# A two-layer hybrid block on one core: gram heads side by side, value products in pairs of key tiles, norm squares by halves, broadcasts by transposes, new stream shares

## The chip, the core and the metric

The kernel runs on one core of a Trainium2 chip. TensorE (PE) multiplies, VectorE (DVE), ScalarE (ACT) and GpSimd (POOL) work elementwise, SyncE (SP) issues the DMAs. The metric is the device time of one execution in microseconds; lower is better. A "clock" is the share of its full 2.4 GHz that TensorE was granted in a stretch.

## What is computed

Two layers over 1,280 tokens (256 of a context, 1,024 latents) of width 1,024, all in float32. Each layer is a modulated RMS norm, one projection w_in into four mixers that see the same tokens, the projection w_out, a second norm and an MLP. Cut to what matters here:

```python
def _rms(x, g):
    y = x * lax.rsqrt(jnp.mean(jnp.square(x), axis=-1, keepdims=True) + EPS)
    return y * g

def gated_delta_rule(q, k, v, g, beta, s0):        # 4 heads of 64, chunks of 64, two directions
    decay = jnp.exp(jnp.where(tri, gc[..., :, None] - gc[..., None, :], -jnp.inf))
    a = jnp.where(strict, jnp.einsum('bhncd,bhnsd->bhncs', k * beta, k) * decay, 0.0)
    t_inv = triangular_solve(a + eye, eye)
    u, w = t_inv @ (v * beta), t_inv @ (k * beta * jnp.exp(gc))
    qk = jnp.where(tri, jnp.einsum('bhncd,bhnsd->bhncs', q, k) * decay, 0.0)
    ...                                            # scan over chunks: v_new = u - w @ s, o = q @ s + qk @ v_new

def _attend(q, k, v):                              # mla: 4 heads, 96 wide, values 64 wide
    p = softmax(jnp.einsum('bqhd,bkhd->bhqk', q, k) * (MLA_QK ** -0.5))
    return jnp.einsum('bhqk,bkhd->bqhd', p, v)

for l in range(DEPTH):
    a = _modulate(h, norm1_g[l], m[0], m[1]) @ w_in[l]
    ya, yb, yc, yd = gdn_mixer(a), s5_mixer(a), mamba2_mixer(a), mla_mixer(a)
    h = h + m[2] * (concatenate([ya, yb, yc, yd]) @ w_out[l])
    h = h + m[5] * _sq_relu_mlp(_modulate(h, norm2_g[l], m[3], m[4]), w_ff1[l], w_ff2[l])
```

The products `q k` and `k k` of the delta rule are called grams below, and the triangular solve is done by a base inverse of 16 x 16 blocks followed by merges.

## The kernel before

**Streams.** The program is written as generators. `Streams.run` always steps the one whose own clock `at` is smallest; a step adds the estimated cost of what it issued, divided by the stream's share:

```python
s = min(ok, key=lambda s: s.at)
...
s.at += (self.work[0] + 20) / s.share
```

The shares stand in the table `SHARE` (lines 147 to 151); a higher share lets a stream get further in the same time. The order that comes out is the order of each engine's queue (a tile framework adds the waits); each engine works its queue in order. Since every instruction is issued through one helper, all carry its line, L125, and groups are told apart by the names of their tiles.

**The main stream** runs per layer: `w_in1` and `w_in2` (projections, weights split into a high and a low part, three products per tile: `a_hi,w_hi`, `a_lo,w_hi`, `a_hi,w_lo`), `ssd`, `mla`, then `s5` if nobody has begun it, then it waits for the side stream, and runs `w_out` and `ffn`. **The side stream** (`beside`, line 1914) starts with share `prep0` and does the small per-token factors, `gdn_prep` of the first pair of heads, then `gdn`: for each of two head pairs the grams and base inverse (`base`), the merges and the scan chains of both directions (`solve`), and at the end `s5`. So the delta rule is interleaved with projections, ssd and mla.

**Banks.** TensorE writes into PSUM banks, named by who uses them: two `mm`, one each of `g`, `x`, `m0`, `m1`, `c0`, `c1`. In the trace `m` and `c` are those of the two directions together. The merges use only `m`, the chains `c`; the base uses `m` and `c` in turn.

**What the change touches:**
- `gram` (481): an exponent of the decay in one bank; then per head `hl` a bank, two products of 64-row operands `qk[hs]` (one per tile of the pair), two scalings on VectorE, and a yield. Base and chain call it, the chain at 646 with three times its bank c.
- `gdn_prep` (415), `ssd` (783), `norm_scale` (1600): a row of per-token factors (`g_cx`, `s_rr`, `n_rr`) is spread over 128 partitions by a product with the identity, `mm(b, x, ident)`.
- `norm_scale`: per 128 tokens ScalarE squares 1,024 rows into `n_sq` (8 x 128 per partition), VectorE sums the eight by one reduce into `n_acc`, TensorE sums over partitions.
- `att` in `mla_att` (1094): per key tile six score products (two heads, three products) into a bank, an exponent on ScalarE into `m_p` (three buffers), running sums on GpSimd, and, two tiles behind, two value products `x<-m_p,m_va` into 64 rows each of the bank `x`. `fin` (1129) sums `m_sum` over partitions and divides.
- `s5`'s output writes `yd`, reads it as `5_yf`, multiplies by `5_wg`, and puts `5_mo` into the mixers' buffer `mx`, from which `w_out` loads `f_mx`.

A matrix product on float32 operands is two records in the trace, a transpose (`tr`) one.

Of the kernel before, what the change touches and what calls it, by code (L numbers as in the profile page):

```python
# [7 lines left out]
F32 = mybir.dt.float32  # L8
# [4 lines left out]
OP = mybir.AluOpType  # L13
AX = mybir.AxisListType
# [99 lines left out]
class Engine:  # L114
# [14 lines left out]
    def cost(self, op, aps):  # L129
# [4 lines left out]
        if self.name == "tensor":  # L134
# [12 lines left out]
SHARE = {"start": 1.2612, "norm": 8.885, "mod": 0.7917, "tables": 2.1733, "conv": 0.1457, "ffn": 5.4917,  # L147
# [3 lines left out]
         "chain": 1.0205, "heads": 1.2072, "scan": 1.1114, "factors": 1.7425}  # L151
# [58 lines left out]
class Core:  # L210
# [204 lines left out]
    def gdn_prep(self, l, getP, hp, pool, p1, G, bk):  # L415

        nc, A, S, c = self.nc, self.A, self.S, self.c
# [21 lines left out]
        for x in range(2):  # L439
# [4 lines left out]
            for t0, n in ((0, 2), (2, 4), (6, 4)):  # L444
                b = self.bank(bk)
                for j in range(n):
                    self.mm(b[:, j * 128:j * 128 + 128], rnx[:, t0 + j].rearrange("p h e -> p (h e)"), c["ident"])
# [14 lines left out]
    def gdn(self, l, getP, put, G, bk, ctx_out=True, side="right"):  # L462
# [18 lines left out]
        def gram(hp, d, qk, p2, x, tags, pool, dtag, dst=None):  # L481
# [19 lines left out]
            yield  # L501
            for hl in range(2):
                g = self.bank(next(tag))
                hs = slice(64 * hl, 64 * hl + 64)
                for i in range(2):
                    oi = o + 128 * i
                    self.mm(g[:, 128 * i:128 * i + 128], qk[hs, 0, oi:oi + 128], qk[hs, x, oi:oi + 128])
                for i in range(2):
                    be = S["beta"][:, t + i, 4 * d + 2 * hp + hl:4 * d + 2 * hp + hl + 1]
                    nc.vector.scalar_tensor_tensor(dst[:, i, hl], g[:, 128 * i:128 * i + 128], be, D[:, i, hl],  # L510
# [124 lines left out]
        def chain(hp, d, p2, V, wT, st, ot, pool, seen):  # L635
# [9 lines left out]
            if t in tiles:  # L645
                qg = yield from gram(hp, d, qk, p2, 1, (f"c{d}",) * 3, pool, f"g_Dq{d}")
# [136 lines left out]
    def ssd(self, l, getP, conv, put, pool, bk, ctx_out=True):  # L783
# [110 lines left out]
        for t0, n in ((0, 2), (2, 4), (6, 4)):  # L894
# [3 lines left out]
            for j in range(n):  # L898
                self.mm(b[:, j * 128:j * 128 + 128], rr[:, t0 + j:t0 + j + 1].to_broadcast([128, 128]), c["ident"])
# [132 lines left out]
    def mla_att(self, put, wk, qt, kt, va, gq, ctx_out, bk, sk, ak):  # L1032
# [61 lines left out]
        def att():  # L1094
            for i in range(2 * len(blocks)):
# [5 lines left out]
                ps = {}  # L1101
                for k in range(nk + 2):
                    if k < nk:
# [7 lines left out]
                        ps[k] = self.t(wk, [128, 512], F32, "m_p", bufs=3)  # L1111
# [3 lines left out]
                    if k == 2 and pend:  # L1115
                        fin(*pend.pop(), acc[:, 256:512])
                    if k >= 2:
                        for x in range(2):
# [993 lines left out]
```

## Time and profile before

| | |
|---|---|
| three runs | 4422.18, 4426.31, 4437.6 us (median 4426.31) |
| the profiled execution | 4413.32 us, span 4411.5 us, mean granted clock 0.919 |
| busy: TensorE, VectorE, GpSimd, ScalarE | 89%, 62%, 33%, 29% of the span |
| layer 0: w_in beside the delta rule | about 300 to 745 us |
| layer 0: ssd | about 745 to 950 us |
| layer 0: mla | about 950 to 1356 us |
| layer 0: w_out, norm, MLP | 1377 to about 2380 us |
| layer 1: mixers, then w_out and MLP | about 2500 to 3580, and 3580 to 4411 us |

Busy time is what the engine spent in instructions; a stretch's clock says how fast TensorE's were. What an engine does alone costs its duration, what it does while the next one is waiting for something else costs nothing; the chain of waits says which engine held up the end at each moment.

### The profile page before, as it was taken

Reading aid. Unit: us, or ns where it says so; the run is one execution under the profiler, and the core shown is the slowest. Engines: PE = TensorE matmul, PEld = TensorE weight load, DVE = VectorE, ACT = ScalarE, POOL = GpSimd, SP = SyncE. Lnnn points to the kernel's source line nnn. Section 1 sums busy time; section 2 is a strip of 40 time slices with the busy share of each in tenths; the row PEclk is TensorE's granted clock in tenths of the full one; section 3 lists DMA queues with packets and bytes.
Section 4 is the critical chain, followed back from the end, with each engine's and each line's share of the span. In section 5 each row is a group of like instructions: output and inputs, shape, how many; then the busy total and the mean of one; then the engine's idle time right before and its main releaser. Section 6 shows DMA issues by size and latency. Waiting matters only on the chain.

```text
span 4411.5 us, 61602 instructions
## 1 busy us (share of the span) xinstructions
PE 3920.8 (89%) x23416; PEld 3135.9 (71%) x23416; DVE 2713.7 (62%) x6343; ACT 1275.3 (29%) x2027; POOL 1449.0 (33%) x1664
## 2 busy tenths in 40 slices
PE   4689897898887899999999799897978998999999
PEld 2466786675665778877788677776855666888887
DVE  7866555756554599997775655576765436444443
ACT  3224235332223321112222343234322233212121
POOL 3432532434452221123332224334435432212121
PEclk8899996787898999999999999996979998999999
DMA  4346333010335022311111233342041230111111
GB/s 184 119 158 188 113 123 104 1 45 3 77 106 174 29 86 96 101 63 54 63 56 56 86 133 104 102 145 67 8 109 35 66 137 29 53 44 54 42 58 58
DMA packets 170872, 367.30 MB, mean 83 GB/s; under 512 B 46160, under 2 KB 88400, under 8 KB 166864
## 3 DMA queue, kind: packets, MB, share of 16 engines
q1 hardware_dynamic: 170576, 363.37, 25.5%
q8 instruction: 184, 3.01, 0.3%
q14 instruction: 112, 0.92, 0.1%
HBM read 277.42 MB, written 85.89 MB: 82 GB/s over the span
## 4 chain that ended last, share of the span: by engine, by line
PE 62%; DVE 23%; POOL 6%; issue 3%; ACT 3%; DMA 2%; SPq 0%; POOLq 0%; DVEq 0%; ACTq 0%
PE mm L125 43%; PE m L125 7%; PE c L125 5%; PE g L125 4%; PE x L125 3%; DVE mod_acc L125 3%; DVE h L125 2%; DVE n_x L125 1%; DVE s_ca L125 1%; DVE 5_t_k L125 1%; POOL g_pr L125 1%; DVE n_acc L125 1%; DVE g_scr L125 1%; POOL a_lo L125 1%; DVE rsq_u L125 1%
## 5 line engine op out<-in xcount | busy, mean ns | idle before, releaser
L125 PE MATMUL mm<-a_hi,w_hi 128*128 128x512 f32 (+1 forms) x2576 | 979.2, 381 | 54.6 <-ACT w_hi L125 20.8
L125 PE MATMUL mm<-a_lo,w_hi 128*128 128x512 f32 (+1 forms) x2576 | 970.3, 377 | 31.9 <-POOL a_lo L125 19.3
L125 PE MATMUL mm<-a_hi,w_lo 128*128 128x512 f32 (+1 forms) x2576 | 964.3, 375 | 1.2 <-POOL w_lo L125 1.2
L125 POOL TENSOR_TENSOR w_lo<-w_raw,w_hi 128x1024 fp32r<-128x1024 f32 x189 | 464.4, 2466 | 1225.7 <-ACT w_hi L125 1225.7
L125 DVE SCALAR_TENSOR_TENSOR h<-mm,md,h 128x512 f32<-128x512 f32 (+1 forms) x680 | 467.2, 692 | 255.1 <-PE mm L125 254.2
L125 PEld LDWEIGHTS mm<-a_hi,w_hi 128*128 128x128 f32 x2576 | 499.4, 194 | 146.9 <-ACT w_hi L125 21.3
L125 PEld LDWEIGHTS mm<-a_lo,w_hi 128*128 128x128 f32 x2576 | 499.2, 194 | 123.0 <-POOL a_lo L125 28.2
L125 PEld LDWEIGHTS mm<-a_hi,w_lo 128*128 128x128 f32 x2576 | 499.2, 194 | 82.5 <-issue 2.4
L125 PE MATMUL mm<-f_rh,w_hi 128*128 128x512 f32 (+1 forms) x1280 | 478.6, 374 | 28.4 <-DVE f_r L125 14.4
L125 PE MATMUL mm<-f_rl,w_hi 128*128 128x512 f32 (+1 forms) x1280 | 474.0, 370 | 0.0
L125 PE MATMUL mm<-f_rh,w_lo 128*128 128x512 f32 (+1 forms) x1280 | 473.8, 370 | 0.0
L125 ACT CAST w_hi<-w_raw 128x1024 fp32r<-128x1024 f32 x234 | 242.4, 1049 | 770.5 <-PE mm L125 636.3
L125 DVE SCALAR_TENSOR_TENSOR f_r<-mm,f_r 128x512 f32<-128x512 f32 (+1 forms) x160 | 101.4, 634 | 360.4 <-ACT f_rh L125 359.7
L125 PEld LDWEIGHTS mm<-f_rh,w_hi 128*128 128x128 f32 x1280 | 244.2, 191 | 72.8 <-DVE f_r L125 16.8
L125 PEld LDWEIGHTS mm<-f_rh,w_lo 128*128 128x128 f32 x1280 | 243.6, 190 | 40.4
L125 PEld LDWEIGHTS mm<-f_rl,w_hi 128*128 128x128 f32 x1280 | 244.0, 191 | 39.1
L125 ACT ACTIVATE f_r<-mm 128x512 f32<-128x512 f32 (+1 forms) x160 | 88.2, 552 | 549.6 <-PE mm L125 461.6
L125 DVE SCALAR_TENSOR_TENSOR mod_acc<-mod_w,cond,mod_acc 128x128 f32<-128x128 f32 x672 | 238.2, 400 | 1.5
L125 POOL TENSOR_TENSOR m_sum<-m_sum,m_p 128x512 f32<-128x512 f32 x128 | 164.5, 1285 | 127.5 <-ACT m_p L125 121.6
L125 DVE SCALAR_TENSOR_TENSOR s_ca<-s_cx,s_prm,s_ca 128x255 f32<-128x255 f32 (+2 forms) x240 | 149.5, 640 | 17.5 <-ACT s_ca L125 15.6
L125 POOL TENSOR_TENSOR a_lo<-n_x,a_hi 128x512 fp32r<-128x512 f32 (+1 forms) x66 | 77.0, 1175 | 184.6 <-DVE n_x L125 172.5
L125 PE MATMUL x<-m_p,m_va 128*64 128x256 f32 x656 | 119.2, 413 | 11.1 <-ACT m_p L125 5.1
(491 smaller groups left out, 6783.4 us busy)
## 6 DMA issues: line engine op xcount, KB each, us to landing
w_raw<-in_w_ff SPq DMA_DIRECT2D x128, 512.0 KB, 3.5
w_raw<-in_w_in SPq DMA_DIRECT2D x90, 512.0 KB, 3.7
mod_w<-in_w_mod SPq DMA_DIRECT2D x80, 512.0 KB, 3.7
pd<-st SPq DMA_DIRECT2D x80, 257.0 KB, 2.4
s5d<-5_fc SPq DMA_DIRECT2D x32, 577.0 KB, 2.8
5_fc<-s5d SPq DMA_DIRECT2D x16, 1154.0 KB, 6.5
g_cx<-pd SPq DMA_DIRECT2D x18, 643.0 KB, 5.3
h<-in_hT SPq DMA_DIRECT2D x4, 2048.0 KB, 10.3
```

Of the source, the lines that this page charges most:

```text
L125: return f(*args, **kw)
```

## The change

Five things: (1) in `gram` both heads' banks are taken first, the four products alternate between the heads (rows 0 to 63 and 64 to 127 of the operands), and the scalings follow; the chain's gram takes the banks c, m, c. (2) Three broadcasts become transposes. (3) In `att` the value products of two key tiles are issued together at every odd step from the third on; `m_p` has four buffers; `fin` comes at step 3. (4) The reduce of the squares becomes three adds of halves. (5) Most shares are set anew.

```diff
-SHARE = {"start": 1.2612, "norm": 8.885, "mod": 0.7917, "tables": 2.1733, "conv": 0.1457, "ffn": 5.4917,
-         "w1_0": 1.0, "w2_0": 1.3776, "prep0_0": 0.4156, "solve0_0": 0.44, "prep1_0": 0.4371, "solve1_0": 0.2483,
-         "mla_0": 0.9161, "ssd_0": 0.8009, "s5_0": 1.1874, "w1_1": 0.8438, "w2_1": 0.9426, "prep0_1": 0.2832,
-         "solve0_1": 0.44, "prep1_1": 0.4243, "solve1_1": 0.6473, "mla_1": 1.156, "ssd_1": 0.8906, "s5_1": 4.1833,
-         "chain": 1.0205, "heads": 1.2072, "scan": 1.1114, "factors": 1.7425}
+SHARE = {"start": 1.4006, "norm": 7.9949, "mod": 0.7917, "tables": 3.0591, "conv": 0.1388, "ffn": 5.4917,
+         "w1_0": 0.9376, "w2_0": 1.3776, "prep0_0": 0.1806, "solve0_0": 0.4513, "prep1_0": 0.4642,
+         "solve1_0": 0.2102, "mla_0": 0.9476, "ssd_0": 0.8009, "s5_0": 1.3121, "w1_1": 0.7053, "w2_1": 0.9426,
+         "prep0_1": 0.2832, "solve0_1": 0.4978, "prep1_1": 0.3746, "solve1_1": 0.6473, "mla_1": 1.3799,
+         "ssd_1": 0.8561, "s5_1": 3.3729, "chain": 1.0205, "heads": 0.4024, "scan": 1.0954, "factors": 2.0471}
...
-                    self.mm(b[:, j * 128:j * 128 + 128], rnx[:, t0 + j].rearrange("p h e -> p (h e)"), c["ident"])
+                    self.tr(b[:, j * 128:j * 128 + 128], rnx[:, t0 + j].rearrange("p h e -> p (h e)"))
...
+            gb = [self.bank(next(tag)) for hl in range(2)]
+            for i in range(2):
+                for hl in range(2):
+                    hs = slice(64 * hl, 64 * hl + 64)
+                    oi = o + 128 * i
+                    self.mm(gb[hl][:, 128 * i:128 * i + 128], qk[hs, 0, oi:oi + 128], qk[hs, x, oi:oi + 128])
             for hl in range(2):
-                g = self.bank(next(tag))
-                hs = slice(64 * hl, 64 * hl + 64)
-                for i in range(2):
-                    oi = o + 128 * i
-                    self.mm(g[:, 128 * i:128 * i + 128], qk[hs, 0, oi:oi + 128], qk[hs, x, oi:oi + 128])
                 for i in range(2):
                     be = S["beta"][:, t + i, 4 * d + 2 * hp + hl:4 * d + 2 * hp + hl + 1]
-                    nc.vector.scalar_tensor_tensor(dst[:, i, hl], g[:, 128 * i:128 * i + 128], be, D[:, i, hl],
+                    nc.vector.scalar_tensor_tensor(dst[:, i, hl], gb[hl][:, 128 * i:128 * i + 128], be, D[:, i, hl],
...
-                qg = yield from gram(hp, d, qk, p2, 1, (f"c{d}",) * 3, pool, f"g_Dq{d}")
+                qg = yield from gram(hp, d, qk, p2, 1, (f"c{d}", f"m{d}", f"c{d}"), pool, f"g_Dq{d}")
...
-                self.mm(b[:, j * 128:j * 128 + 128], rr[:, t0 + j:t0 + j + 1].to_broadcast([128, 128]), c["ident"])
+                self.tr(b[:, j * 128:j * 128 + 128], rr[:, t0 + j:t0 + j + 1].to_broadcast([128, 128]))
...
-                        ps[k] = self.t(wk, [128, 512], F32, "m_p", bufs=3)
+                        ps[k] = self.t(wk, [128, 512], F32, "m_p", bufs=4)
...
-                    if k == 2 and pend:
-                        fin(*pend.pop(), acc[:, 256:512])
-                    if k >= 2:
-                        for x in range(2):
-                            self.mm(acc[64 * x:64 * x + 64, 0:256], va[:, k - 2, 2 * pr + x, :],
-                                    ps[k - 2][:, 256 * x:256 * x + 256], start=k == 2, stop=k == nk + 1)
-                    yield
+                    if k % 2 and k > 1:
+                        if k == 3 and pend:
+                            fin(*pend.pop(), acc[:, 256:512])
+                        for j in (k - 3, k - 2):
+                            for x in range(2):
+                                self.mm(acc[64 * x:64 * x + 64, 0:256], va[:, j, 2 * pr + x, :],
+                                        ps[j][:, 256 * x:256 * x + 256], start=j == 0, stop=j == nk - 1)
+                    if k < nk or k % 2:
+                        yield
...
-            nc.vector.tensor_reduce(acc[:, hf:hf + 128], sq.rearrange("p k w -> p w k"), AX.X, OP.add)
+
+            for n in (4, 2, 1):
+                nc.vector.tensor_tensor(acc[:, hf:hf + 128].unsqueeze(1) if n == 1 else sq[:, 0:n], sq[:, 0:n], sq[:, n:2 * n],
+                                        op=OP.add)
...
-            self.mm(b[:, 128 * t:128 * t + 128], rr[:, t:t + 1].to_broadcast([128, 128]), self.c["ident"])
+            self.tr(b[:, 128 * t:128 * t + 128], rr[:, t:t + 1].to_broadcast([128, 128]))
```

How this moves the instructions is seen at three places. First TensorE's queue in layer 0, beside the projections, where a gram of one direction stands. Before (`m` and `c` are banks, the numbers tell their uses apart, x2 is two products in a row):

```order
L125 MATMUL mm<-a_hi_736,w_hi 128x256
L125 MATMUL mm<-a_lo_737,w_hi 128x256
L125 MATMUL mm<-a_hi_736,w_lo 128x256
L125 MATMUL c_5777<-g_qk 128x128 x2
L125 MATMUL c_5782<-g_qk 128x128 x2
L125 MATMUL mm<-a_hi_736,w_hi 128x256
L125 MATMUL mm<-a_lo_737,w_hi 128x256
L125 MATMUL mm<-a_hi_736,w_lo 128x256
```

And after, where both directions' grams meet:

```order
L125 MATMUL mm<-a_hi_4175,w_lo 128x512
L125 MATMUL m_5420<-g_qk 128x128
L125 MATMUL c_5421<-g_qk 128x128
L125 MATMUL m_5420<-g_qk 128x128
L125 MATMUL c_5421<-g_qk 128x128
L125 MATMUL m_5428<-g_qk 128x128
L125 MATMUL c_5429<-g_qk 128x128
L125 MATMUL m_5428<-g_qk 128x128
L125 MATMUL c_5429<-g_qk 128x128
L125 MATMUL mm<-a_hi_4175,w_hi 128x512
L125 MATMUL m_5436<-g_TU_5360,g_xs_5376 64x64 x8
```

Two heads that stood behind each other now alternate between bank m and bank c.

Second, TensorE's queue in attention of layer 1, near its end, where nothing else cuts in (`m_khi`, `m_klo`, `m_qhi`, `m_qlo` are the high and low parts of keys and queries, `m_va` the values). Before, and then after:

```order
L125 MATMUL x<-m_p,m_va 64x256 x2
L125 MATMUL mm<-m_qhi,m_khi 128x256
L125 MATMUL mm<-m_qlo,m_khi 128x256
L125 MATMUL mm<-m_qhi,m_klo 128x256
L125 MATMUL mm<-m_qhi,m_khi 128x256
L125 MATMUL mm<-m_qlo,m_khi 128x256
L125 MATMUL mm<-m_qhi,m_klo 128x256
L125 MATMUL x<-m_p,m_va 64x256 x2
```

```order
L125 MATMUL mm<-m_qhi,m_klo 128x256
L125 MATMUL mm<-m_qhi,m_khi 128x256
L125 MATMUL mm<-m_qlo,m_khi 128x256
L125 MATMUL x<-m_p,m_va 64x256 x8
L125 MATMUL mm<-m_qhi,m_klo 128x256
L125 MATMUL mm<-m_qhi,m_khi 128x256
```

The value products of one tile stood after every six score products; now those of several tiles stand together.

Third, the end of layer 0's mixers on TensorE: `5_p`, `5_U` and `5_fc` are s5's mixing, `5_yf,5_wg` its gate, and `mm<-a_hi,w_hi` the first product of w_out. Before, s5's gate stands amid attention:

```order
L125 MATMUL mm<-m_qhi,m_klo 128x256
L125 MATMUL m_11401<-5_yf,5_wg 128x256 x2
L125 MATMUL c_11411<-5_yf,5_wg 128x256 x2
L125 MATMUL x<-m_p,m_va 64x256 x2
L125 MATMUL mm<-m_qhi,m_khi 128x256
```

and after:

```order
L125 MATMUL c_11856<-5_p_11752,5_fc 128x160
L125 MATMUL c_11856<-5_p_11753,5_E_11749 128x160
L125 MATMUL x<-m_p,m_va 64x256
L125 MATMUL x<-m_sum,ctab 64x256 x2
L125 MATMUL m_11930<-5_yf,5_wg 128x512 x2
L125 MATMUL c_11948<-5_yf,5_wg 128x512 x2
L125 MATMUL m_12004<-5_yf,5_wg 128x512 x2
L125 MATMUL c_12023<-5_yf,5_wg 128x512 x2
L125 MATMUL m_12059<-5_yf,5_wg 128x256 x2
L125 MATMUL c_12092<-5_yf,5_wg 128x256 x2
L125 MATMUL mm<-a_hi_12320,w_hi 128x512
```

Here the gate stands behind attention's last product, between it and w_out. On SyncE's queue six loads of w_out's weights (`w_raw<-in_w_out`) now stand ahead of the loads `f_mx<-mx`; before, the first stood behind twelve of them.

## Rows read from the trace of the kernel before

**Rows 1.** The page: busy time of two engines, and the chain by engine

```profile
PE 3920.8 (89%) x23416; PEld 3135.9 (71%) x23416; DVE 2713.7 (62%) x6343; ACT 1275.3 (29%) x2027; POOL 1449.0 (33%) x1664
...
PE 62%; DVE 23%; POOL 6%; issue 3%; ACT 3%; DMA 2%; SPq 0%; POOLq 0%; DVEq 0%; ACTq 0%
PE mm L125 43%; PE m L125 7%; PE c L125 5%; PE g L125 4%; PE x L125 3%; DVE mod_acc L125 3%; DVE h L125 2%; DVE n_x L125 1%; DVE s_ca L125 1%; DVE 5_t_k L125 1%; POOL g_pr L125 1%; DVE n_acc L125 1%; DVE g_scr L125 1%; POOL a_lo L125 1%; DVE rsq_u L125 1%
```

**Rows 2.** Stretches: length; busy PE, PEld, DVE, ACT, POOL; granted clock, DMA share, GB/s

```profile
450.00:600.00 150.00, 135.84 (x1648) 122.03 (x1647) 80.55 (x182) 44.64 (x78) 67.12 (x93) 0.94 0.30 104
...
745.00:960.00 215.00, 185.63 (x1563) 153.73 (x1561) 131.28 (x398) 78.19 (x133) 83.60 (x142) 0.79 0.07 23
...
1060.00:1200.00 140.00, 127.42 (x654) 85.46 (x655) 68.19 (x162) 42.70 (x73) 61.77 (x58) 0.81 0.27 63
...
1500.00:1560.00 60.00, 48.87 (x222) 41.13 (x223) 49.82 (x113) 24.04 (x37) 13.30 (x12) 0.85 0.09 27
```

**Rows 3.** The chain of waits within 745 to 960 us, by engine and bank

```profile
by line: PE m L125 21.5%; PE mm L125 17.8%; PE c L125 11.9%; PE g L125 9.6%; PE x L125 7.8%; POOL g_pr L125 3.7%; POOL s_ysum L125 3.5%; DVE s_st L125 3.2%; DVE g_ax L125 2.0%; issue 1.7%; ACT g_cx L125 1.3%; POOL g_TU L125 1.2%; POOL s_bd
```

**Rows 4.** Waits of TensorE: us in total, times, longest

```profile
PE g L125 <- DVE n_acc L125: 66.7, 20, 18.0
```

**Rows 5.** Timeline of TensorE, grams: start, us of the group, records

```profile
411.17 0.71 PE L125 MATMUL m<-g_qk 64*128 64x128 f32 x4
411.80 0.49 PE L125 MATMUL mm<-a_hi,w_hi 128*128 128x512 f32 x1
...
413.30 1.16 PE L125 MATMUL c<-g_qk 64*128 64x128 f32 x8
414.38 0.51 PE L125 MATMUL mm<-a_hi,w_lo 128*128 128x512 f32 x1
...
428.79 0.37 PE L125 MATMUL m<-g_qk 64*128 64x128 f32 x1
428.89 0.27 PE L125 MATMUL c<-g_qk 64*128 64x128 f32 x1
...
429.23 0.72 PE L125 MATMUL m<-g_qk 64*128 64x128 f32 x5
```

**Rows 6.** The chains' scaled tiles: duration ns min/median/max, first and last start

```profile
L125 DVE SCALAR_TENSOR_TENSOR g_Dq<-c,sm_beta,g_Dq x144: 330/343/352, 482.2 to 3226.6; 128x128 f32<-128x128 f32 x144
```

**Rows 7.** A broadcast by product, and transposes in TensorE's timeline

```profile
400.92 0.27 PE L125 MATMUL m<-ctab,g_scr 128*128 128x128 f32 x1
401.03 0.27 PE L125 MATMUL c<-ctab,g_qk 128*128 128x128 f32 x1
...
L125 PE MATMUL g<-ctab,n_rr x76: 275/275/552, 43.7 to 3708.3; 128*128 128x128 f32 x76
```

**Rows 8.** Timeline of TensorE in layer 0's attention

```profile
1291.70 0.65 PE L125 MATMUL x<-m_p,m_va 128*64 128x256 f32 x4
1292.29 0.38 PE L125 MATMUL g<-m_qhi,m_khi 97*128 97x256 f32 x1
1292.51 0.28 PE L125 MATMUL g<-m_qlo,m_khi 97*128 97x256 f32 x1
1292.63 0.28 PE L125 MATMUL g<-m_qhi,m_klo 97*128 97x256 f32 x1
```

**Rows 9.** The norms: VectorE's reduce and multiply, and GpSimd's subtraction

```profile
L125 DVE TENSOR_REDUCE n_acc<-n_sq x38: 1855/1943/2020, 13.0 to 3700.2; 128x128 f32<-128x1024 f32 x38
...
L125 DVE TENSOR_TENSOR n_x<-h,n_acc x88: 409/682/2869, 60.0 to 3723.1; 128x512 f32<-128x512 f32 x64, 128x256 f32<-128x256 f32 x24
...
L125 POOL TENSOR_TENSOR a_lo<-n_x,a_hi 128x512 fp32r<-128x512 f32 (+1 forms) x66 | 77.0, 1175 | 184.6 <-DVE n_x L125 172.5
```

**Rows 10.** Timelines of SyncE and TensorE at the end of layer 0's mixers

```profile
1275.41 12.06 SPq L125 DMA_DIRECT2D yd<-5_U  x24
...
1358.76 0.32 SPq L125 DMA_DIRECT2D mx<-m_o  x1
...
1377.25 0.80 PE L125 MATMUL mm<-a_hi,w_hi 128*128 128x512 f32 x1 [20.85 <-ACT w_hi L125]
```

## The prediction

> **What bounds the kernel now.** I read first the page's busy table and its chain [rows 1]: TensorE is busy 89% of the span, VectorE 62%, and the chain that ended last is TensorE for 62%, VectorE for 23%, GpSimd for 6%. So a microsecond of TensorE work is worth something less than a microsecond. Then I asked for the stretches [rows 2], since the touched work lies only in some of them. The mixer stretches are 86 to 91% busy on TensorE, with a granted clock of 0.79 to 0.94 of 2.4 GHz. The chain within one of them [rows 3] is TensorE for 69%, by five banks in turn: this is no single gemm but many short chains interleaved on one in-order queue. The two ffn stretches (some 1,500 us) hold none of the change but the norms ahead of them; whatever the change brings must come from some 2,900 us. Then the waits of TensorE [rows 4], where one group that the change touches stands out: products that wait for the norm's sums of squares, 66.7 us in 20 waits. The rest came from single instructions in the timeline.
>
> The profiled execution took 4413.3 us (span 4411.5), 13 us below the median of the three runs, 4426.3. The sum is made against the profiled one, and the difference is carried to the median.
>
> **Gram heads side by side.** A gram is four products of 64-row operands, two records each. One head alone holds TensorE 0.63 us (411.17 to the next product at 411.80), both heads in one bank one after the other 1.08 (413.30 to 414.38) [rows 5]. Records of one bank follow each other by 0.11 us, so 4 records are 0.44 and 8 are 0.88, and some 0.20 goes on changing over to such operands and back. The same rows show what two heads on different halves of the array do when they alternate between two banks: in before that happens by accident, where the two directions meet. From 428.79 to 429.23 four records of bank m pass, and those of bank c pass in between (428.89). A gram side by side is then 0.44 + 0.20 = 0.64 us, in place of 2 x 0.63 = 1.26 or 1.08: 0.44 to 0.62 us less. There are 76 grams (2 layers x 2 head pairs x 2 directions x 5 in the base, 40; the chains have 36, since layer 1 leaves the context tile pair out: the 144 scalings of rows 6 are four per gram). All of them saved would be 33 to 47 us. Some already overlap as at 428.79, so I take 28; the bounds are 47 and, if the alternation doesn't overlap once the scheduler has placed it, 0. The order of after shows the four alternating in a row, which speaks for the gain.
>
> **Broadcasts by transposes.** 38 for the norms (76 records, rows 7), 80 for the reciprocal norms of q and k and 18 in ssd make 136 products of two records. A transpose is one record, and two of them in a row start 0.11 us apart (400.92, 401.03) [rows 7]. One record less each: 136 x 0.11 = 15 us of TensorE. Bounds: 0 (if a lone transpose costs its changeover anyway) and 15.
>
> **Values of two key tiles together.** The value products of a key tile are four records; they hold TensorE 0.59 us, 0.44 of it records, and the first score product after them takes 0.22 us to the next one where the others take 0.12 [rows 8]. So a visit costs some 0.25 to 0.34 us beyond its records. The 164 key tiles (84 in layer 0, 80 in layer 1) make 82 pairs, so at most 82 visits (28 us) go. In the order, though, the value products stood in 142 separate groups before and stand in 112 after, since other streams cut in between and also gather tiles in before: 30 x 0.34 = 10 us. The exponents gain a fourth buffer, and a score tile is held one step longer; with scores in two banks I give that nothing.
>
> **Norm squares.** One reduce of 1024 elements takes 1.94 us, 38 times [rows 9]. Three adds of 512, 256 and 128 take its place: the two forms of the nearest two-input multiply are 512 and 256 wide, at 0.68 and 0.41 us [rows 9], and a straight line gives 0.27 for 128, in sum 1.36. That is 0.58 less on VectorE, 22 us for all. On the path only a part counts: n_acc has 1% of the chain [rows 1], some 44 us, of which 0.58/1.94 is 13. The same row has one multiply at 2.87 us, so two-input instructions are at times held up. I take -6; ends -13 and, for the rival below, +50.
>
> **The shares.** They move whole streams, and the order shows two moves that can be priced. In layer 0 the first head pair's solve goes later: of the 1,040 merge products 520 stood beside w_in2, 304 beside ssd and 216 beside mla; now 312, 208 and 520. TensorE is busy nine tenths there and here, so most of it only changes its place. Bank m has 21.5% of the chain in ssd's stretch of 215 us [rows 3], 46 us for 304 products; the 208 that leave w_in2 are 31 us, and go from a stretch at 0.94 to one at 0.81 [rows 2]: 31 x (0.94/0.81 - 1) = 5 us lost. Ends -15 and +15, for waits that I can't order. Second, s5 of layer 0 now mixes while mla ends: 148 of the 168 value products of attention stand ahead of s5's first mix (88 before) and 167 ahead of the last. So s5's output is no longer covered by mla. Before, its 24 writes (12.06 us on SyncE) run from 1275.41, beside attention, and w_out starts 18.5 us after the last attention output is issued (1358.76, 1377.25), with TensorE idle for 20.85 us of it and of the time just before [rows 10]. After, writes, a read, the gate and those 18.5 us stand in a row behind attention: 12.1 + 18.5, and some five dependent steps at the 0.7 us of the wide multiply, 3.5, make 34. That the weights of w_out are now issued ahead of those loads, not behind them, may pay for the read, which I have not counted. 34 - 21 is +13 us; ends 0 and +25. Queued behind SyncE's writes are the loads of w_out's input, and all of TensorE waits for these. The norms of the start and layer 1 keep their places, and I give the rest of the shares nothing.
>
> **The sum.** TensorE work: 28 + 15 + 10 = 53 us at full clock. The stretches in which it lies had 0.79 to 0.94 [rows 2], so 53/0.87 = 61 us; of that 0.65 counts (between 62% of the whole chain and 69% in the mixer stretch): -40. Norms -6, end of layer 0 +13, moved solve +5: -28. From 4426 that is 4398 us.
>
> **The rivals.** *The rows give more.* All grams and all 82 visits gain, 47 + 15 + 28 = 90 us, 103 at that clock, x 0.65 = 67, and the tail is hidden: 67 + 6 = 73, 4353 us. For it: the mixer stretches are bound by TensorE. Against: the order still shows 112 groups, and s5's rows stand at the end.
>
> *The time saved turns into waits.* The four short chains are bound by what answers TensorE, not by TensorE: 31% of the mixer chain is VectorE, GpSimd and ScalarE [rows 3]. If a third of the 61 us counts, 20, the sum is -20 - 6 + 18 = -8: 4418. For it: after every gram VectorE needs 4 x 0.34 us [rows 6], as before. Against: TensorE is at nine tenths.
>
> *Bank m becomes the stop.* The chains' grams (36) took their three banks from c alone and now take c, m, c. Bank m is the merges' only one, and it is held for the products, 0.64 us, and the two scalings of its head, 2 x 0.34 [rows 6]: 1.33 us. TensorE's queue is in order: a merge product that waits for m holds all gemm, ssd and mla products behind it. If each of the 36 does, that is 48 us, and the time 4446. It outweighs the rest from 28/36 = 0.8 us per gram. For it: m and c have 33% of the mixer chain [rows 3], so merges come thickly. Against: other products stand between a gram and the next merge in the order, and before the second head had to wait for c in the same way.
>
> *The adds are held up.* VectorE's slowest two-input multiply took 2.87 us where the median is 0.68 [rows 9]; GpSimd's subtractions that run beside norms read SBUF for 1.18 us each [rows 9]. If each tree meets one such hold, 38 x 2.2 = 83 us, of which 44/73.5 lies on the path: +50, the time 4398 + 6 + 50 = 4454. Against: the norms' stretch has GpSimd busy 13 of 60 us [rows 2], so a hold of this length meets few trees. The Trainium skill ("SBUF — State Buffer", Who interferes with whom) says why it could be: a VectorE instruction with two SBUF inputs contends with a GpSimd instruction that reads SBUF, a reduce never does. By that rule the adds pay where the reduce did not, and this trace agrees so far that the reduce stays within 1.86 to 2.02 us and the multiplies spread from 0.41 to 2.87.
>
> *The change does less than it says*: the transposes cost their changeover and the grams overlapped already; with 15 and 18 us of the 53 gone the sum is -15 - 6 + 18 = -3: 4423. This I count with the waits.
>
> **How the numbers follow.** A measurement of this kernel can tell about 0.3%, 13 us, from no change. Forecast (4370 to 4413) 0.56; more than that (around 4353) 0.13; waits or less effect (4413 to 4440) 0.20; bank m 0.08; held-up adds 0.03. Faster is then 0.56 + 0.13 = 0.69, same 0.20, slower 0.11. The likeliest case gives 4398. The range leaves out one in ten at either end: 4350 below, by the larger gain, and 4440 above, where the two slower rivals begin.
>
> **What would show each step.** Grams: records of m and c on g_qk alternating, 0.11 us apart, and the chains' exponents no longer followed by two separate visits. Bank m: waits of TensorE's m for the scaled tile. Broadcasts: one record each, TensorE's records fewer by 136. Values: groups of eight records of m_p where four stand now, at most one visit per two tiles. Norms: the three adds at some 0.7, 0.4 and 0.3 us, and a shorter wait than 66.7 us. Layer 0's end: a gap of 30 us or more between the last value product and the first of w_out where 20.85 stood [rows 10]. I am wrong if TensorE's busy time falls by 50 us and the span doesn't follow, or if the span falls by far more than TensorE's busy time does, since then the shares, which I gave almost nothing, made the difference.

## The result, and the profile after

The changed kernel took 4324.4 us (median of four runs, 4311.0 to 4328.2), before 4428.4 in the same session: a ratio of 0.976 (95% interval 0.973 to 0.979), or 104 us. I had forecast 4398 us, 28 us less than before, and a range of 4350 to 4440. The direction was right and the size was not.

The profiled execution of after has a span of 4309.2 us. From its page, what answers to [rows 1]:

```profile
PE 3817.7 (89%) x23280; PEld 3058.1 (71%) x23280; DVE 2716.2 (63%) x6419; ACT 1259.1 (29%) x2015; POOL 1455.5 (34%) x1664
...
PE 46%; DVE 15%; POOL 3%; DMA 2%; ACT 2%; issue 2%; SPq 0%; DVEq 0%; ACTq 0%; POOLq 0%
```

TensorE's busy time fell by 103 us and the span by 102, as if a microsecond of TensorE were a microsecond of time. That reading is wrong, and the clock says so. (The chain's shares sum to 70% only: it could be followed back to about 1,300 us, so it can't be set against before.) Span and granted clock, first of after, then of before:

```profile
core 0: 4309.2 us, clock 0.931
```

```profile
core 0: 4411.5 us, clock 0.919
```

The clock in both traces is either full or half, and the same instruction takes about twice as long at half: 512-wide projection products start 227 ns apart at full clock and 427 ns at half (medians in before). So TensorE's busy time is split here into *work* (time at half clock counted half), *half clock* (the other half of that time) and *idle*; the three add up to the span. Before has 3678 + 242 + 491 us, after 3632 + 186 + 491: by these two traces 46 us of the 102 are work, 57 are clock, and the waits in sum did not change. The stretches show where (length; busy PE, PEld, DVE, ACT, POOL; clock; DMA share, GB/s). First after, in layer 0: w_in beside the delta rule, ssd, then attention to the solve's end, to attention's last product, and to the start of w_out:

```profile
383.10:638.40 255.30, 234.31 (x1983) 195.53 (x1982) 157.36 (x320) 101.28 (x158) 108.45 (x142) 0.95 0.50 157
638.40:851.50 213.10, 167.56 (x1125) 138.05 (x1125) 152.98 (x431) 85.79 (x133) 82.86 (x121) 0.79 0.13 44
...
948.70:1116.50 167.80, 163.99 (x1501) 123.64 (x1501) 93.52 (x236) 55.53 (x101) 73.21 (x80) 0.97 0.03 9
1116.50:1264.90 148.40, 131.85 (x857) 94.04 (x855) 86.56 (x194) 34.11 (x60) 87.62 (x125) 0.98 0.37 104
1264.90:1314.00 49.10, 13.38 (x29) 6.29 (x25) 14.24 (x15) 16.02 (x19) 9.76 (x4) 0.67 0.66 187
```

The same places of before: w_in beside the delta rule, ssd, then attention to the solve's end and, in two parts, to attention's end:

```profile
396.30:755.40 359.10, 319.85 (x2592) 270.70 (x2589) 215.56 (x475) 135.44 (x202) 148.85 (x182) 0.89 0.37 121
755.40:951.00 195.60, 166.23 (x1477) 138.62 (x1476) 126.58 (x382) 68.03 (x123) 78.56 (x137) 0.80 0.08 26
...
1047.70:1111.30 63.60, 60.98 (x292) 38.94 (x292) 33.25 (x77) 16.07 (x29) 21.41 (x20) 0.84 0.05 15
1111.30:1201.60 90.30, 78.67 (x425) 53.88 (x424) 44.13 (x101) 29.66 (x49) 42.14 (x40) 0.81 0.38 87
1201.60:1356.00 154.40, 132.72 (x800) 89.52 (x800) 74.85 (x150) 44.97 (x72) 79.28 (x114) 0.94 0.34 102
```

The stretch beside w_in is 104 us shorter, ssd 17 longer. Attention took 308 us and takes 316, although 520 merge products in place of 216 stand beside mla: it ran at 0.81 to 0.94 and runs at 0.97 and 0.98. Its work is 288 us in place of 240, its half clock 8 in place of 32, its idle time 20 in place of 36. The tail, from attention's last product to w_out, that I had priced at 34 us is 49. In all w_out starts 63 us earlier, the attention of layer 1 ends 101 us earlier, and from there on nothing changes (841 and 840 us).

Stage times come from one profiled execution each. e10 and e11 below have TensorE's instructions in after's order all through layer 0, and yet attention ends there at 1271 and 1285 us in place of 1265. So a start or an end in a single trace tells little under some 20 us; lengths of stages and gaps scatter less. After's profile lies 13 us below the median of its runs, before's 15 us, e11's 17 above.

The edits themselves, in after. Two grams, each with four products, in TensorE's timeline (start, us, records), against [rows 5]:

```profile
596.88 0.37 PE L125 MATMUL m<-g_qk 64*128 64x128 f32 x1
596.89 0.37 PE L125 MATMUL c<-g_qk 64*128 64x128 f32 x1
...
597.77 0.27 PE L125 MATMUL m<-g_qk 64*128 64x128 f32 x1
597.77 0.27 PE L125 MATMUL c<-g_qk 64*128 64x128 f32 x1
598.36 0.45 PE L125 MATMUL m<-g_TU,g_xs 64*64 64x64 f32 x8 [0.32 <-DVE g_Dq L125]
```

Sixteen records, eight in each bank, pass in 0.89 us from the first start to the last. Two grams hold TensorE 1.16 us (596.88 to 598.36, less the wait of 0.32) where one alone took 1.08. The norm squares, the broadcasts, and TensorE's wait that was 66.7 [rows 4, 7, 9]:

```profile
L125 DVE TENSOR_TENSOR n_sq<-n_sq x76: 405/550/2039, 13.1 to 3599.6; 128x512 f32<-128x512 f32 x38, 128x256 f32<-128x256 f32 x38
...
L125 DVE TENSOR_TENSOR n_acc<-n_sq x38: 272/284/483, 14.3 to 3600.6; 128x128 f32<-128x128 f32 x38
...
L125 PE MATMUL g<-ctab,n_rr x38: 272/417/476, 43.1 to 3606.1; 128*128 128x128 f32 x38
...
PE g L125 <- DVE n_acc L125: 65.4, 10, 17.7
```

The first row mixes two widths; apart, their medians are 0.69 and 0.42 us, so the tree is 0.69 + 0.42 + 0.28 = 1.4 us, as costed. The wait hardly changed.

### The profile page after: what moved, and what is told of

Its sections match the earlier page's. It is cut to its first block, busy times and chain, and to the rows that moved or that the text cites. A ratio compares the mean times of both kernels' runs of the same rounds, so it can differ in the third digit from the quotient of the medians.

```text
span 4309.2 us, 61386 instructions
## 1 busy us (share of the span) xinstructions
PE 3817.7 (89%) x23280; PEld 3058.1 (71%) x23280; DVE 2716.2 (63%) x6419; ACT 1259.1 (29%) x2015; POOL 1455.5 (34%) x1664
## 4 chain that ended last, share of the span: by engine, by line
PE 46%; DVE 15%; POOL 3%; DMA 2%; ACT 2%; issue 2%; SPq 0%; DVEq 0%; ACTq 0%; POOLq 0%
PE mm L125 38%; PE m L125 3%; DVE mod_acc L125 3%; PE g L125 2%; PE c L125 2%; DVE h L125 2%; DVE n_x L125 1%; PE x L125 1%; DVE s_ca L125 1%; POOL a_lo L125 1%; POOL g_pr L125 1%; DVE g_scr L125 1%; DVE rsq_u L125 1%; SPq L125 0%; DVE f_r L125 0%
## 5 line engine op out<-in xcount | busy, mean ns | idle before, releaser
L125 DVE TENSOR_TENSOR f_rl<-f_r,f_rh 128x512 fp32r<-128x512 f32 (+1 forms) x160 | 116.1, 726 | 2.0
```

The lines of the kernel that those rows point to most:

```text
L125: return f(*args, **kw)
```

## The experiments

Before is 4426 to 4430 us in each comparison, and after, measured above, 4324. The theories A to G stand in the expectations, which were written before each run.

**Edits or shares?** e1 has the code of after with the table of before, e2 the code of before with the table of after (both tables stand in the change). e3 is after with one share set back, e4 before with the same share set as in after:

```diff
-"prep0_0": 0.1806
+"prep0_0": 0.4156
```

```diff
-"prep0_0": 0.4156
+"prep0_0": 0.1806
```

> The four edits of the code with the table of shares of before. Theory A (the shares brought most of the unforecast gain, by moving the first head pair's solve beside attention in layer 0, where TensorE's clock had been 0.81): here only the work saved is left, so 4385 to 4395 us, a ratio of about 0.991 to before, and the stretch from 1048 to 1200 us keeps a clock near 0.82. Theory B (the edits themselves bring more than I costed): about 4340 us, 0.98. Theory C (only both together give it): within 0.3% of before.

Measured: 4418.4 us, 0.998 (0.996 to 1.000).

> The code of before with the table of shares of after. Theory A: 4360 to 4380 us, a ratio of 0.985 to 0.99, attention's clock in layer 0 near 0.97 from its start, and a gap of some 50 us ahead of w_out. Theory B: 4420 to 4450 us, since the tail of s5 is then uncovered and nothing pays for it. Theory C: within 0.3% of before.

Measured: 4384.0 us, 0.991 (0.989 to 0.993).

> After, with one share set back: prep0_0 = 0.4156 in place of 0.1806, which puts the first head pair's solve back beside w_in2 and s5 of layer 0 back beside attention. Theory A: some 50 us slower than after, 4375 us, the first value product of layer 0 back near 1040 us, the clock of attention's first 150 us back near 0.82. Theory B: within 15 us of after (the tail of s5 covered again, -28, against what little the place of the solve is worth).

Measured: 4371.3 us, 0.987 (0.985 to 0.990).

> Before, with one share changed: prep0_0 = 0.1806 in place of 0.4156; the solve of the first pair goes late as in after. Here s5 of layer 0 stands wholly behind attention, so a tail of some 60 us or more is uncovered. Theory A: faster than before all the same, 4380 to 4410 us, with a high clock in attention. Theory B: slower than before, 4440 to 4480 us, by the tail.

Measured: 4458.4 us, 1.007 (1.004 to 1.009).

The edits alone give 9 us, the shares alone 44, both 104: adding does not work. A is near on e2 and e3 and fails on e1 and e4; the tail that B names decides e4 (131 us there); C holds on e1 and fails on e2. One share, prep0_0, costs before 31 us and is worth 47 in after. The split of one trace each (us, rounded; e11, below, has nearly after's order, so the distance of the last two rows is what one execution differs from another):

| kernel | span | work | half clock | idle |
|---|---|---|---|---|
| before | 4412 | 3678 | 242 | 491 |
| e1, edits alone | 4421 | 3632 | 261 | 528 |
| e2, shares alone | 4382 | 3676 | 221 | 484 |
| after | 4309 | 3632 | 186 | 491 |
| e11, nearly after | 4340 | 3634 | 226 | 480 |

The work does add up: the edits save 46 us of it on the old shares and 44 on the new, the shares 2 at most. On the old shares 37 us of the 46 come back as waits of TensorE, more than the last two rows differ (11 us); the 18 of half clock are within what these two differ (40). One trace is too little for the clock; the means of all runs are steadier (product: span times clock; e1 has twelve runs, and its trace is 9 us longer than before's where its median is 9 shorter):

| kernel | mean span | clock | product | span less product |
|---|---|---|---|---|
| before | 4424 | 0.917 | 4057 | 367 |
| e1, edits alone | 4417 | 0.912 | 4028 | 389 |
| e2, shares alone | 4385 | 0.923 | 4048 | 337 |
| after | 4320 | 0.9285 | 4011 | 309 |

The product counts TensorE's idle time at half clock half as well (227 of 712 us at half clock in before, 222 of 594 in after), though a wait need not shrink with the clock; so the differences of the last column tell more than its size. The edits add 22 us to it on the old shares and take 28 from it on the new. After has four runs only, with clocks of 0.925 to 0.932; e11's seven runs have 326 us there, by which it would be 11.

**Which edit?** After with one edit undone at a time, by the lines of the change read backwards. e5 (gram one head after the other):

```diff
-            gb = [self.bank(next(tag)) for hl in range(2)]
...
+                g = self.bank(next(tag))
...
-                qg = yield from gram(hp, d, qk, p2, 1, (f"c{d}", f"m{d}", f"c{d}"), pool, f"g_Dq{d}")
+                qg = yield from gram(hp, d, qk, p2, 1, (f"c{d}",) * 3, pool, f"g_Dq{d}")
```

e6 (one key tile per step, three buffers), e7 (one reduce) and e8 (products at all three broadcasts, the last of which is shown):

```diff
-                    if k % 2 and k > 1:
...
+                    if k >= 2:
```

```diff
-            for n in (4, 2, 1):
...
+            nc.vector.tensor_reduce(acc[:, hf:hf + 128], sq.rearrange("p k w -> p w k"), AX.X, OP.add)
```

```diff
-            self.tr(b[:, 128 * t:128 * t + 128], rr[:, t:t + 1].to_broadcast([128, 128]))
+            self.mm(b[:, 128 * t:128 * t + 128], rr[:, t:t + 1].to_broadcast([128, 128]), self.c["ident"])
```

> After, with the gram of before (one head after the other, the chain's bank c alone). Theory D (under the new shares the delta rule and s5 end together with attention in layer 0, so whatever lengthens the delta rule's chain is paid in full, and TensorE's clock follows): 40 to 50 us slower than after, 4365 to 4375 us, the solve of layer 0 ending some 30 us later than 1116 us. Theory E (the edits add up as work saved, with no regard to place or clock): about 28 us slower, 4350 us.

Measured: 4335.1 us, 0.979 (0.977 to 0.981): 11 slower than after.

> After, with the value products of each key tile alone again and three buffers. Theory D: attention of layer 1 longer by its 80 visits x 0.3 us, 15 to 25 us in all. Theory E: 10 us slower than after, which the interval hardly tells from none.

Measured: 4353.6 us, 0.983 (0.981 to 0.985): 29 slower.

> After, with the one reduce of the squares again. Theories D and E: 6 to 13 us slower, all of it in the first 390 us and ahead of the two second norms. If two-input adds are held up by GpSimd, no difference or a few us faster.

Measured: 4331.9 us, 0.978 (0.976 to 0.980): 8 slower.

> After, with the 136 broadcasts as products again. By work alone (theory E) 13 us slower. The products also count more in the streams' costs, so the order changes: s5 of layer 0 then mixes wholly behind attention, as in the run with the shares alone. Theory D: 25 to 45 us slower, with a tail ahead of w_out of 60 to 90 us in place of 49.

Measured: 4356.7 us, 0.984 (0.982 to 0.987): 32 slower, with a tail of 88 us in place of 49.

Grams lie below both theories and, like the norms, are hardly clear of the noise; values lie above D's 15 to 25 us, broadcasts within D's range, with the tail that D foresaw. Broadcasts by products cost more on the streams' own counters `at`, so e8 also has another order; its 32 us are not the price of 136 records. Grams: summed over TensorE's timeline, from the first record of a visit to the next other product and with waits taken off, they hold TensorE 102 us in before, 67 in after and 86 in e5; with time at half clock counted half that is 82, 64 and 84. Values, counted in the same way at full clock: 103 in before, 102 in after, 111 in e6. Layer 1's attention is 236 us in e6 and 227 in after, layer 0's is 330 and 316 (321 in e11).

**What ends layer 0?** The stages of the kernels so far give a rule that I had not seen before: w_out starts at the later of attention's last product plus 21 us, and the solve's end plus some 200 us for s5 and its output. To test it, e9 gives more of TensorE to the side stream, e11 spreads s5's writes over two queues, and e12 has both edits; e10 sets layer 1's own shares back. All start from after. e9, e11 and e10:

```diff
-"mla_0": 0.9476
+"mla_0": 0.85
```

```diff
-                nc.sync.dma_start(self.yd[l][i].rearrange("(g c) (s j) -> s c g j", c=16, s=8)[s],
+                (nc.sync if i == 1 else nc.scalar).dma_start(self.yd[l][i].rearrange("(g c) (s j) -> s c g j", c=16, s=8)[s],
```

```diff
-"w1_1": 0.7053, "solve0_1": 0.4978, "prep1_1": 0.3746, "mla_1": 1.3799, "ssd_1": 0.8561, "s5_1": 3.3729
+"w1_1": 0.8438, "solve0_1": 0.44, "prep1_1": 0.4243, "mla_1": 1.156, "ssd_1": 0.8906, "s5_1": 4.1833
```

> After, with one share changed: mla_0 = 0.85 in place of 0.9476, so attention of layer 0 yields more of TensorE to the delta rule and s5 beside it. Theory F (w_out of layer 0 starts at the later of two ends: the delta rule's solve plus some 195 us for s5 and its output, or attention's end plus some 21 us; in the changed kernel the first is the later one, in the kernel before the second): solve ends 10 to 25 us sooner, attention some 20 us later, w_out 10 to 20 us sooner; 4305 to 4315 us. Theory G (TensorE is full, and the order among full streams is worth nothing): within 8 us of the changed kernel's 4324.

Measured: 4315.4 us (4311.9 to 4318.8), 0.975 (0.973 to 0.977). The time is at the edge of F's range and 9 us off G's 4324, but w_out starts where it did, at 1313 us, with the solve's end 5 us sooner in place of 10 to 25. So e9 does not confirm the rule's forecast.

> After, with the six shares that act in layer 1 alone set back (w1_1, solve0_1, prep1_1, mla_1, ssd_1, s5_1). If the new shares carry layer 1's gain of 34 us: 4340 to 4360 us, the stretch of layer 1's mixers near 890 to 905 us in place of 871, and layer 0 as it was. If the edits carry it: 4320 to 4330 us.

Measured: 4337.8 us, 0.980 (0.978 to 0.982), between the two expectations. Layer 1's mixers take 885 us in place of 871.

> After, with 16 of the 24 writes of s5's output issued from ScalarE's queue in place of SyncE's. The 24 writes took 12.2 us of SyncE's queue at the head of the uncovered tail. If the tail is that chain (theory F): the first gate product 6 to 8 us sooner, w_out 4 to 8 us sooner, 4317 to 4320 us, which the interval hardly tells. If something else is late next there: no change.

Measured: 4325.2 us, 0.976 (0.974 to 0.979): no change.

> Both of the two edits before: mla_0 = 0.85 and the writes from two queues. Theory F: they add up as long as the side stream is the later one, so 4298 to 4310 us, faster than the changed kernel. Theory G: within 8 us of 4324.

Measured: 4350.6 us, 0.982 (0.980 to 0.984): slower than after, against both theories.

In one table, from the traces (layer 0, start of three products: the chains' last one on `g_qk`, which stands 1 to 4 us ahead of the solve's very last, attention's last, w_out's first):

| kernel | solve | attention | w_out | from solve | from attention |
|---|---|---|---|---|---|
| before | 1111 | 1356 | 1377 | 266 | **21** |
| e1 edits alone | 1107 | 1352 | 1374 | 267 | **22** |
| e3 after, prep0_0 back | 1089 | 1346 | 1368 | 278 | **21** |
| e12 mla_0 0.85, two queues | 1110 | 1312 | 1333 | 223 | **21** |
| after | 1117 | 1265 | 1314 | **198** | 49 |
| e2 shares alone | 1162 | 1271 | 1358 | **196** | 88 |
| e4 before, prep0_0 late | 1229 | 1281 | 1412 | **183** | 131 |
| e5 / e7 gram, norms back | 1129 / 1125 | 1281 / 1274 | 1331 / 1323 | **202 / 198** | 50 / 50 |
| e6 / e8 values, broadcasts back | 1129 / 1144 | 1292 / 1248 | 1341 / 1336 | **212 / 192** | 49 / 88 |
| e9 / e11 mla_0 0.85, two queues | 1111 / 1130 | 1279 / 1285 | 1313 / 1330 | **202 / 200** | 35 / 45 |
| e10 layer 1's shares back | 1123 | 1271 | 1321 | **198** | 50 |
| e14 edits and heads (below) | 1061 | 1325 | 1347 | 286 | **21** |
| e13 / e15 (below) | 1165 / 1130 | 1219 / 1299 | 1346 / 1347 | **181 / 218** | 127 / 49 |

The five kernels that attention ends wait 21 to 22 us behind it. In the others the side stream is the later one, with 181 to 218 us from the solve; that is a range and no constant, and why it spreads was not taken apart. That explains e4: prep0_0 alone makes attention early and the solve late. With edits and shares the solve is as early as before, 1117 against 1111, beside an attention that ends 91 us earlier.

It does not explain e1. There the solve and attention end 5 us sooner than in before, which is scatter, so layer 0 gains next to nothing. What the edits lose on the old shares they lose above all in ssd of layer 1 (before, then e1):

```profile
3029.90:3246.60 216.70, 187.12 (x1866) 159.13 (x1866) 148.43 (x445) 72.53 (x134) 83.73 (x148) 0.83 0.07 25
3022.30:3263.00 240.70, 193.99 (x1867) 165.55 (x1866) 152.12 (x453) 77.27 (x139) 86.81 (x153) 0.79 0.10 34
```

It is 229 to 241 us in the four kernels with the edits on layer 1's old shares (e1, e10, e14, e15), 217 on the same shares without the edits (before), and 204 in after. Why it is longer was not traced.

e11 hardly shortened the tail (45 against 49), and e12 shows what that queue costs. ScalarE's timeline in each (ACTq is its DMA issue), e11 first, with SyncE's issues of the same time:

```profile
1283.80 7.25 SPq L125 DMA_DIRECT2D yd<-5_U  x8
1283.94 16.79 ACTq L125 DMA_DIRECT2D yd<-5_U  x16
1300.84 1.28 ACT L125 ACT_TABLE_LOAD   x1 [16.59 <-DMA w_raw<-in_w_out]
```

```profile
1263.64 15.25 ACTq L125 DMA_DIRECT2D yd<-5_U  x16
1280.53 1.28 ACT L125 ACT_TABLE_LOAD   x1 [16.91 <-DMA yd<-5_U]
```

In both, 16 issues hold ScalarE longer than all 24 held SyncE in after, 12.2 us; and SyncE's own eight take 7.25 us beside them, 0.9 us each in place of 0.5. In e12 attention is not over: its exponents stand behind the issues, TensorE idles 16 us ahead of s5's gate (1282.93), the gate then goes first, and ScalarE, which alternates between exponents and s5's functions, loads its function tables (ACT_TABLE_LOAD, 1.28 us each) eight times from 1250 to 1315 us, four times in e9. Attention ends 33 us later than in e9. The Trainium skill ("DMA: Bandwidth & Descriptors", Rules for kernel authors) says that spreading DMAs over issuing engines only saves issue time; here it saved none.

**Which other share?** One more group, of the share that sets attention's preparation (`heads`) against attention itself. e13 is after with it set back; e14 is e1, the edits on the table of before, with it as in after; e15 is e14 with prep0_0 as in after too (the second and third cut are against e1's table):

```diff
-"heads": 0.4024
+"heads": 1.2072
```

```diff
-"heads": 1.2072
+"heads": 0.4024
```

```diff
-"heads": 1.2072, "prep0_0": 0.4156
+"heads": 0.4024, "prep0_0": 0.1806
```

> After, with one share set back: heads = 1.2072 in place of 0.4024 (attention's preparation of queries and keys against attention itself, in both layers). If the heads' share carries attention's part: layer 1's attention 237 to 243 us in place of 227, as in the runs without either the paired values or the new shares, and in layer 0 attention ends earlier but the side stream's solve later, with w_out later by 10 us or more; 4345 to 4365 us. If not: within 8 us of 4324.

Measured: 4376.6 us, 0.988 (0.986 to 0.990): 52 slower than after, more than expected.

> The edits with the shares of before and heads = 0.4024 alone. Layer 0 is still bound by attention's end, so the gain of attention itself is seen in both layers: 227 to 232 us in layer 1 in place of 243, and 10 us sooner in layer 0; 4390 to 4405 us against 4418 for the edits with all shares of before. If the heads' share does nothing alone: 4415 to 4422.

Measured: 4378.1 us, 0.989 (0.987 to 0.990): 40 faster than the edits alone, more than expected.

> The edits with the shares of before and two of after, heads = 0.4024 and prep0_0 = 0.1806. If these two and the edits make the change, with the rest of the shares worth the 13 us of layer 1's six: 4335 to 4355 us, w_out of layer 0 at 1315 to 1335 us, the solve's end 195 to 202 us before it. If the other shares matter as much: 4370 us or more.

Measured: 4374.0 us, 0.988 (0.986 to 0.989): by the second expectation, the other shares matter as much.

The heads' share is the largest of the three that were tried singly in after (prep0_0, mla_0, heads). Layer 1's attention in e1 and then in e14, the same code but for that number:

```profile
3337.10:3580.00 242.90, 218.47 (x1341) 149.35 (x1340) 122.19 (x243) 76.85 (x126) 129.24 (x157) 0.94 0.24 78
```

```profile
3297.40:3524.70 227.30, 210.83 (x1329) 144.13 (x1328) 121.91 (x243) 74.66 (x123) 128.26 (x156) 0.96 0.26 83
```

Idle time falls from 24 to 16 us and busy time from 218 to 211, with the clock two points up. It is 241 us in e13 and 242 in e2 (old values), 236 in e6: paired values alone give 4 of the 20 us, the new shares alone 5 to 10, both 20, and e13 says that of the shares it is this one. Why attention runs closer when its preparation gets a smaller share was not taken apart further. In layer 0 of e14 the solve ends 45 us and attention 26 us earlier than in e1. With prep0_0 added (e15) the solve ends at 1130 and w_out starts where it did, at 1347; that the remaining shares of layer 0 (solve0_0, solve1_0, prep1_0, w1_0, mla_0, s5_0) are not set for it is likely and not shown, since none of them but mla_0 was tried alone. Layer 1's mixers in all took 905 us in before, 917 in e1, 883 in e2, 871 in after, and 885 in e10 and 886 in e13: its own six shares and the heads' are some 14 us each. Up to the first gram before, e1 and e2 take 395 to 396 us, after takes 383, and the kernels that differ from after in one place 385 to 390. These 6 to 13 us also need edits and shares together and were not traced further.

## Why the prediction was wrong, point by point

In the terms of my sum, the edits were put at -46 us (work -40, norms -6) and the shares at +18 (tail +13, moved solve +5, the rest nothing). Alone, the edits measured -9 and the shares -44; beside each other -60 (4384 to 4324) and -94 (4418 to 4324). The shares had the wrong sign: that is the step that failed most, and the factor from work to time is the second.

**Work saved on TensorE: about right.** The 53 us at full clock were 44 to 46. Of these grams, put at 28, are 18 (82 to 64); the other 17 us that they hold TensorE less (102 to 67) are clock. Broadcasts lost their 136 records, put at 15; e8 has 6 us more work than after. Values were put at 10 and are 1 between before and after, 9 between e6 and after: I counted groups between the old order and the new, 142 and 112, but under the new shares the single products stand in 157 (e6). e6 is 29 us slower all the same, so most of that is not work on those products. Norms were put at 6, e7 says 8, inside its interval of some 9 us to either side.

**The factor from work to time: the wrong step.** I divided by the clock of before, 0.87, as if the clock stayed, and let 0.65 of the work count wherever it stood. The same edits lowered the mean clock from 0.917 to 0.912 on the old shares and raised it from 0.923 to 0.9285 on the new, and 46 us of work were worth 9 us there and 60 here. In e1's trace TensorE's waits grew by 37 us, and over the runs span less product by 22; that the waits brought the lower clock is likely, not shown. The rival that the time saved turns into waits (4418) was meant for the whole change, so that its number is that of the edits alone (4418.4) is luck; its mechanism is what the edits alone show.

**"I give the rest of the shares nothing": the step that failed most.** I had priced the two moves that the order showed and passed over a factor of three in `heads`, since its products stayed in the same stages. It is worth 52 us in after (e13) and 40 beside the edits alone (e14).

**The moved solve: wrong sign.** I let it move from a stretch at 0.94 to one at 0.81 and lose 5 us, taking the clock as a property of the place. It was not: attention beside the moved merges and grams ran at 0.97 (164 of 168 us busy, the third row of after's stretches), and up to the solve's end at 0.90 to 1.00 in all thirteen kernels with that prep0_0. What sets it the rows don't say; busy time alone does not, since before was 96% busy at 0.84 in the same place (61 of 64 us) and after 89% at 0.98. e3 prices the move with its tail at 47 us.

**The tail: right mechanism, too small.** s5's output did come to stand uncovered, and the table shows it as the thing that ends layer 0 in after. I had +13, it was +28 (49 against 21). TensorE's timeline there (in brackets the idle time before and what ended it):

```profile
1264.62 0.65 PE L125 MATMUL x<-m_sum,ctab 128*64 128x256 f32 x4 [0.46 <-ACT m_o L125]
1284.33 3.78 PE L125 MATMUL m<-5_yf,5_wg 128*128 128x512 f32 x4 [19.06 <-ACT 5_yf L125]
...
1305.09 2.07 PE L125 MATMUL m<-5_yf,5_wg 128*128 128x256 f32 x4 [11.54 <-ACT 5_yf L125]
...
1313.98 0.80 PE L125 MATMUL mm<-a_hi,w_hi 128*128 128x512 f32 x1 [5.12 <-ACT a_hi L125]
```

I had left out that the gate comes in two rounds: the third block's read needs a buffer of the first and stands behind w_raw's loads in SyncE's queue, and that is the second wait, 11.5 us. I had also put the whole solve's place against the tail as separate terms, when the later of two ends was the question.

**The rivals.** Bank m never became the stop: TensorE waited with m for the chains' scaled tile (`g_Dq`) 4.1 us in six waits in all of after. Two-input adds were held up at times, as the multiplies were: of 38 wide adds 35 took 0.67 to 0.69 us and three 0.86, 1.75 and 2.04. Each of the three ran beside a subtraction of GpSimd with two inputs in SBUF and ended 0.55 us behind it. This agrees with the Trainium skill's rule ("SBUF — State Buffer", Who interferes with whom) that a VectorE instruction with two SBUF inputs contends with a GpSimd instruction that reads SBUF; but e7 shows no loss by it. My last test, "the shares made the difference if the span falls by far more than TensorE's busy time", was ill made: busy time falls as the clock rises, and so it matched the span without being its cause.

## What to carry to other kernels

Where two streams share a queue and join, find which one joins later, before pricing anything: here a new balance alone was worth more than the edits alone (44 us against 9). That an edit to the earlier one is worth nothing follows from the rule and was not tried by itself, and whether mla_0 = 0.85 is a better balance still (4315 us against 4324) the overlapping intervals leave open. Split busy time by the granted clock before comparing it. A number that only sets an order can outweigh all the edits beside it, so ask of each what it moves within a stage, not only between stages.

## What had not been expected of the hardware

The clock carried some 41 to 58 of 104 us (367 us of span less product in before, 309 in after, 326 in e11). One order of instructions does not have one clock: attention behind the solve in layer 0 ran at 0.98 in after's trace (148 us) and at 0.90 in e11's (155 us) with the same order on TensorE. Two grams on different halves of the rows and in two banks ran 16 records in 0.89 us, so the overlap holds for whole grams at 0.11 us per record of each bank. And two queues that issue these small writes at once slow each other: SyncE alone took 0.5 us for each (24 in 12.2 us), and beside ScalarE 0.9 (8 in 7.25 us, in which ScalarE issued eight of its own), so that the pair issued hardly faster than SyncE alone.
